# First token rows loaded as one tile of 48 rows; turned tokens split into fp16 parts straight from PSUM

## The chip, the cores and the metric

The kernel runs on one core of a Trainium2 chip. The metric is the device time of one execution in microseconds (us), the median of several runs. A core has five engines that run side by side, each in the order of its own instruction stream: PE (TensorE, matrix products and transposes into PSUM; PEld is its loading of the stationary operand), DVE (VectorE), ACT (ScalarE), POOL (GpSimd) and SP (SyncE, which here only issues DMAs). ACT issues DMAs too, and POOL. TensorE's clock has two levels, 1.2 and 2.4 GHz; the profile gives the granted share, 0.5 or 1.0.

## The reference, cut to what matters

One inference step of a one-layer mixer over 16 meta tokens, 32 sample tokens and 512 prompt tokens of width 2048:

```python
hn   = rmsnorm(h, pre_norm_w)                  # every token row, over 2048 features
proj = einsum('btd,de->bte', hn, w_in)         # 2048 -> 8192: q|f|i|gate | B|C|x|gate
...  # group A: gated linear recurrence over the tokens; group B: width-3 convolution
mix  = einsum('bte,ed->btd', concat(o, yb), w_out)
h    = h + rmsnorm(mix, post_norm_w)
```

The change touches only the way from the token rows `h` in HBM to the turned (feature-major) and normed tokens `hn` in SBUF, the right operand of the first product.

## The kernel before, in words

**Tokens.** The 560 tokens are worked on in two halves of 280 columns: per half 8 meta tokens and 16 sample tokens (24 "first" rows) and 256 prompt rows. The first rows lie in the tile `xs` of 56 rows, the second half's 24 from row 32 on (L105); rows 24 to 31 are never loaded, and so the whole tile is cleared first (L119). Six loads of 8 rows each, issued on ACT's DMA queue (L177 to 180), bring them in. The 512 prompt rows lie in four tiles `xp0` to `xp3` of 128 rows (L181 to 189), on SP's DMA queue between the first weights.

**Weights.** `w_in` comes in blocks of 1024 by 128 in float32 (`raw`, six buffers). For each pair of column blocks there are four: keys "11", "12", "21", "22" (first digit: column block; second: which half of the 2048 rows). `squares` (L249) sums their squares on ACT, `scale_of_weights` (L255) turns the sum into a power-of-two scale, with a small product `pss` on PE, and `split_w` (L273) writes a high fp16 part (ACT) and a low one (DVE).

**Norm.** `norm_x` (L348) squares one half of the features of a token tile on ACT and the other on DVE, works out the scale in small steps on DVE with one root on ACT, and scales the tile in place on DVE.

**Turning.** `turn_x(hf, k)` (L364), k from 0 to 15, turns 128 features of one half: three transposes on PE into one PSUM tile of 280 columns (24 + 128 + 128), an evacuation by ACT to the float32 tile `bf` (a view of `big`) with the norm weight as scale, and for every second k a cast of two k to the high fp16 part on POOL (L377) and a subtraction for the low part on DVE (L378). The results are `xo`, the x operand of all products (`x_b` in the trace). The PSUM tiles come from two pools of two buffers, so four are in flight.

**The product.** `plain` (L393) adds three fp16 matmuls for one k (high by high, high by low, low by high; L306 to 310). In the first loop (L397 to 406) `plain` runs `LAG` = 4 values of k behind `turn_x(0, k)`; at k = 3 the second weight block is split and at k = 6 `xp2` is normed. After it come the squares and splits of the two next weight blocks (L407 to 411), then a loop of `plain` with `turn_x(1, ...)` (L412) and another (L426). From there on the products of all other column blocks follow, then the output product.

**Order.** Everything that goes through `V`, `A`, `G`, `T` (DVE, ACT, POOL, PE) keeps the order of the program on its engine up to L432; DMA issues are placed by the framework's scheduler on their queue. `keep_busy` (L205) gives PE products of the identity without use, eight at the very start (L209) and eight more after `squares(0, ("11",))` (L384); they depend on no load.

Of the kernel before, what the change touches and what calls it, by code (L numbers as in the profile page):

```python
# [8 lines left out]
F32 = mybir.dt.float32  # L9
# [5 lines left out]
AF = mybir.ActivationFunctionType  # L15
ALU = mybir.AluOpType
# [3 lines left out]
P = 128  # L20
D = 2048
KT = D // P
SEQ = 512
# [13 lines left out]
KC = 8  # L37
TH = TOK // 2
# [23 lines left out]
def hymba_kernel(  # L62
# [14 lines left out]
    nc = tc.nc  # L77
    V, A, G, T = (_InOrder(tc, e) for e in (nc.vector, nc.scalar, nc.gpsimd, nc.tensor))
# [15 lines left out]
    bf = big.rearrange("p (h k t) -> p h k t", h=2, k=KT)  # L94
# [5 lines left out]
    def xop(n):  # L100
        return [xo[n][:, i] for i in range(2)]

    pre = ExitStack()
    xr = pre.enter_context(tc.tile_pool(name="xr", bufs=1))
    xs = xr.tile([56, D], F32, name="xs")  # L105
    xp = [xr.tile([P, D], F32, name=f"xp{i}") for i in range(4)]

    ident = const.tile([P, P], F32, name="ident")
    make_identity(nc, ident)
    epst = const.tile([P, 1], F32, name="epst")  # L110
    V.memset(epst, EPS)
    mask = const.tile([P, 8, W], U8, name="mask")
# [3 lines left out]
    wpr = xr.tile([16, P], F32, name="wpr")  # L116
    rest = const.tile([32, P], F32, name="rest")
    V.memset(rest, 0.0)
    V.memset(xs, 0.0)  # L119

    w2d = w_in[0]
    units = [(g * 1024 + i * P) for i in range(H) for pr in PAIRS for g in pr[0:2]]
# [1 line left out]
    raws = {}  # L124
# [7 lines left out]
    def load_w(p, key):  # L132

        i, j = int(key[0]) - 1, int(key[1]) - 1
        raw = wpool.tile([P, KC, P], F32, name=f"raw{key}_{p}", tag="raw", bufs=6)
        c0 = units[2 * p + i]
        src = w2d[j * KC * P:(j + 1) * KC * P, c0:c0 + P]
        nc.sync.dma_start(raw, src.rearrange("(k p) e -> p k e", p=P))
        raws[p, key] = raw
# [35 lines left out]

    xsm = x_sample.rearrange("b t d -> (b t) d").rearrange("(g h r) d -> h g r d", h=2, r=8)
    for hf in range(2):  # L177
        nc.scalar.dma_start(xs[32 * hf:32 * hf + 8], meta_tokens[8 * hf:8 * hf + 8])
        for g in range(2):
            nc.scalar.dma_start(xs[32 * hf + 8 + 8 * g:32 * hf + 16 + 8 * g], xsm[hf, g])  # L180
    nc.sync.dma_start(xp[0], x_prompt[0, 0:P])  # L181
    nc.sync.dma_start(wpr, pre_norm_w[0].rearrange("(r c) -> r c", c=P))
    load_w(0, "11")
    nc.sync.dma_start(xp[1], x_prompt[0, P:2 * P])
    load_w(0, "12")
# [14 lines left out]
    wsc = par[:, 96:112]  # L200
    sxk = par[:, 112:116]
    A.activation(par[:, 127:128], epst, AF.Sqrt)
    warm = ps_mm.tile([P, SEQ], F32, name="warm", tag="mm")

    def keep_busy(n):  # L205
        for _ in range(n):
            T.matmul(warm[:, 0:P], ident, ident, start=True, stop=True)

    keep_busy(8)  # L209
    pt = ps_o.tile([P, SEQ], F32, name="pt_pre", tag="o")  # L210

    def cw(j, c):
# [20 lines left out]
    def scale_of_tokens():  # L233


        t = par[:, 116:117]
        T.transpose(pt[:, 0:16], wpr, ident[0:16, 0:16])
        V.tensor_copy(wpre, pt[:, 0:16])
        V.tensor_reduce(t, wpre, axis=AX.X, op=ALU.max, apply_absolute_value=True)
        V.tensor_tensor(t, t, t, op=ALU.mult)  # L240
        T.transpose(pt[0:1, 128:256], t, ident)
        m = par[0:1, 117:118]
        V.tensor_reduce(m, pt[0:1, 128:256], axis=AX.X, op=ALU.max)
        T.matmul(pt[:, 256:257], ones[0:1, :], m, start=True, stop=True)
        power(sxk[:, 0:1], pt[:, 256:257], float(0x5F3759DF + (8 << 23)))
        V.tensor_scalar(wsc, wpre, sxk[:, 0:1], None, op0=ALU.mult)
        V.tensor_scalar(sxk[:, 1:2], sxk[:, 0:1].bitcast(I32), -1.0, float(381 << 23), op0=ALU.mult, op1=ALU.add)

    def squares(p, keys):  # L249
        t = sws.setdefault(p, wpool.tile([P, 8], F32, name=f"sq_{p}", tag="sq", bufs=4))  # L250
        for key in keys:
            c = ("11", "12", "21", "22").index(key)
            A.activation(junk, raws[p, key].rearrange("p k e -> p (k e)"), AF.Square, accum_out=t[:, c:c + 1])  # L253
# [94 lines left out]
    def norm_x(x, n, i):  # L348

        s0, z, r = rst[:n, 0, i:i + 1], rst[:n, 1, i:i + 1], rst[:n, 2, i:i + 1]  # L350
        A.activation(junk[:n], x[:, 0:D // 2], AF.Square, accum_out=ssp[:n, i, 0:1])
        V.scalar_tensor_tensor(junk2[:n], x[:, D // 2:D], 1.0, x[:, D // 2:D], op0=ALU.mult,
                               op1=ALU.mult, accum_out=ssp[:n, i, 1:2])
        V.tensor_tensor(s0, ssp[:n, i, 0:1], ssp[:n, i, 1:2], op=ALU.add)
        A.activation(r, s0, AF.Sqrt, bias=epst[0:n], scale=1.0 / D)
        V.tensor_scalar(z, s0, -0.5 / D, -0.5 * EPS, op0=ALU.mult, op1=ALU.add)
        V.reciprocal(r, r)
        V.scalar_tensor_tensor(z, r, z, r, op0=ALU.mult, op1=ALU.mult)
        V.scalar_tensor_tensor(r, z, 1.5, r, op0=ALU.add, op1=ALU.mult)
        for c in range(2):  # L360
            c = slice(c * D // 2, (c + 1) * D // 2)
            V.tensor_scalar(x[:, c], x[:, c], r, None, op0=ALU.mult)

    def turn_x(hf, k):  # L364
        pool, tag = ((ps_tr, "tr"), (ps_lv, "lv"))[k % 2]
        ps = pool.tile([P, SEQ], F32, name=f"xt{hf}_{k}", tag=tag)[:, 0:TH]
        ks = slice(k * P, (k + 1) * P)
        a = 32 * hf
        T.transpose(ps[:, 0:24], xs[a:a + 24, ks], ident[a:a + 24, a:a + 24])
        for b in range(2):  # L370
            T.transpose(ps[:, 24 + b * P:24 + (b + 1) * P], xp[2 * hf + b][:, ks], ident)
        A.activation(bf[:, hf, k, :], ps, AF.Copy, scale=wsc[:, k:k + 1])
        if k % 2:
            n = f"b{1 + k // KC}{1 + hf}"
            kk = slice((k - 1) % KC, (k - 1) % KC + 2)
            h, l = xop(n)
            G.tensor_copy(h[:, kk], bf[:, hf, k - 1:k + 1])  # L377
            V.tensor_tensor(l[:, kk], bf[:, hf, k - 1:k + 1], h[:, kk], op=ALU.subtract)  # L378

    scale_of_tokens()  # L380
    norm_x(xs, 56, 0)
    norm_x(xp[0], P, 1)
    squares(0, ("11",))
    keep_busy(8)  # L384
    norm_x(xp[1], P, 2)
    squares(0, ("12",))
    sc0 = scale_of_weights(0, (0, 2))
# [5 lines left out]
    def plain(o, a, hf, k):  # L393
        xn = f"b{1 + k // KC}{1 + hf}"
        mmk(o, ws[0, f"{a}{1 + k // KC}"], xop(xn), k % KC, 0, k == 0, k == KT - 1)

    LAG = 4  # L397
    for k in range(KT + LAG):
        if k < KT:
            turn_x(0, k)  # L400
        if k == 3:
            split_w(0, "12", raws[0, "12"])
        if k == 6:
            norm_x(xp[2], P, 3)
        if k >= LAG:
            plain(f0[0], "1", 0, k - LAG)
    squares(0, ("21", "22"))  # L407
# [4 lines left out]
    for k in range(KT):  # L412
        plain(f0[1], "2", 0, k)
        if k >= 4:
            turn_x(1, k - 4)
        if k == 2:
            lt = ps_o.tile([P, SEQ], F32, name="pt_lb", tag="o")
            T.transpose(lt[:, 32:40], lbp, ident[0:8, 0:8])
            V.tensor_copy(lb, lt[:, 32:40])
# [6 lines left out]
    for k in range(KT):  # L426
        if k < 4:
            turn_x(1, 12 + k)
        if k in (4, 8, 12):
            next(steps1)()  # L430
        plain(f0[2], "1", 1, k)
    V, A, G, T = nc.vector, nc.scalar, nc.gpsimd, nc.tensor  # L432
# [453 lines left out]
    op = ctx.enter_context(tc.tile_pool(name="op", bufs=1, side="right"))  # L886
# [168 lines left out]
    for dp in range(ND):  # L1055
# [3 lines left out]
        for j in range(4 * dp, 4 * dp + 4):  # L1059
            pool, tag = ((ps_mm, "mm"), (ps_x, "x"))[j % 7 >= 3]  # L1060
# [83 lines left out]
```

## Time and profile before

| | us |
|---|---|
| median of 3 runs | 1107.26 (1104.17 to 1107.37) |
| the profiled execution, its own time | 1106.25 |
| span of its trace (first to last instruction) | 1104.5 |
| PE busy | 1045.8 (95%) |
| DVE busy | 585.1 (53%) |
| ACT busy | 525.1 (48%) |
| POOL busy | 89.0 (8%) |
| DMA, mean | 99 GB/s, 109.38 MB |

Times in rows are us from the span's start unless marked ns. "[5.15 <-DMA xs]" behind a row means that the engine stood still for 5.15 us before it and that this transfer ended last of what it waited for. SPq and ACTq rows are the issuing of a DMA, not its transfer.

### The profile page before, as it was taken

What the parts mean: (1) busy time and instruction counts of PE and PEld (TensorE: products, weight loads), DVE (VectorE), ACT (ScalarE), POOL (GpSimd) and SP (SyncE); (2) the same over time, 40 slices, a digit from 0 to 9 for tenths busy, and PEclk for the clock granted to TensorE, in tenths of its full rate; (3) what the DMA queues carried; (4) which work ended last, traced back from release to release, by engine and by line L of the source; (5) the groups of instructions that cost most, each with busy time, mean ns of one, the idle gap of its engine ahead of it and who ended that gap; (6) DMA issues with size and microseconds to landing.
All of it is one profiled execution on the core that took longest, in us unless ns stands there. A gap on an engine that the chain in (4) does not pass through costs nothing.

```text
span 1104.5 us, 20854 instructions
## 1 busy us (share of the span) xinstructions
PE 1045.8 (95%) x8639; PEld 893.8 (81%) x8639; DVE 585.1 (53%) x1403; ACT 525.1 (48%) x1012; POOL 89.0 (8%) x151
## 2 busy tenths in 40 slices
PE   2589999999999999999999999999999999999995
PEld 2357888888788888878888888888788799999995
DVE  2755564466447554743664565557546662223226
ACT  1568744554554455445544554564455152332323
POOL 0220000000001000100001010001000010000004
PEclk7689999999999999999999999999999999999998
DMA  9214423323422244235223333432253154222204
GB/s 261 78 41 129 120 77 97 98 77 80 115 77 78 80 127 130 56 85 143 77 77 98 96 77 80 115 93 63 78 154 98 57 183 164 88 96 88 66 1 162
DMA packets 156949, 109.38 MB, mean 99 GB/s; under 512 B 3745, under 2 KB 151378, under 8 KB 155782
## 3 DMA queue, kind: packets, MB, share of 16 engines
q1 hardware_dynamic: 152934, 92.90, 30.1%
q0 software_dynamic: 3680, 14.49, 4.1%
q8 instruction: 67, 1.10, 0.4%
q10 hardware_dynamic: 240, 0.66, 0.2%
q14 instruction: 28, 0.23, 0.1%
HBM read 98.79 MB, written 9.25 MB: 98 GB/s over the span
## 4 chain that ended last, share of the span: by engine, by line
PE 74%; DVE 12%; DMA 7%; ACT 4%; issue 2%; POOL 0%; SPq 0%; DVEq 0%; ACTq 0%; POOLq 0%
PE mm L308 17%; PE mm L310 16%; PE mm L309 16%; DMA raw<-in_w_in_dram 6%; PE omm L952 3%; PE omm L950 3%; PE omm L951 3%; PE omm L959 2%; PE omm L960 2%; PE omm L958 2%; DVE w L277 2%; PE xt L58 2%; PE mm L58 1%; DVE q L673 1%; DVE y L837 1%
## 5 line engine op out<-in xcount | busy, mean ns | idle before, releaser
L308 PE MATMUL mm<-x_b,w 128*128 128x272 f16 (+2 forms) x2000 | 560.8, 280 | 1.4 <-ACT f L325 1.4
L310 PE MATMUL mm<-x_b,w 128*128 128x272 f16 (+2 forms) x2000 | 560.1, 280 | 0.0
L309 PE MATMUL mm<-x_b,w 128*128 128x272 f16 (+2 forms) x2000 | 560.1, 280 | 0.0
L308 PEld LDWEIGHTS <-w 128*128 128x128 f16 x2000 | 195.6, 98 | 42.3 <-issue 4.8
L310 PEld LDWEIGHTS <-w 128*128 128x128 f16 x2000 | 195.6, 98 | 37.9
L309 PEld LDWEIGHTS <-w 128*128 128x128 f16 x2000 | 195.7, 98 | 35.6
L253 ACT ACTIVATE junk<-raw 128x1024 bf16<-128x1024 f32 x120 | 126.9, 1058 | 115.3 <-DMA raw<-in_w_in_dram 115.2
L277 DVE SCALAR_TENSOR_TENSOR w<-raw,sc,w 128x1024 f16<-128x1024 f32 x124 | 153.4, 1277 | 26.0 <-ACT w L276 25.8
L276 ACT ACTIVATE w<-raw,sc 128x1024 f16<-128x1024 f32 x124 | 133.5, 1142 | 21.4 <-DVE sc L231 19.5
L170 DVE TENSOR_TENSOR wl<-rawo,wh 128x1024 fp32r<-128x1024 f32 x32 | 39.2, 1225 | 81.4 <-ACT wh L169 80.7
L950 PE MATMUL omm<-mh,wh 128*128 128x288 f32 x256 | 76.0, 297 | 0.0
L952 PE MATMUL omm<-mh,wl 128*128 128x288 f32 x256 | 75.5, 295 | 0.0
L951 PE MATMUL omm<-ml,wh 128*128 128x288 f32 x256 | 75.3, 294 | 0.0
L958 PE MATMUL omm<-wh,mh 128*128 128x256 f32 x256 | 72.7, 284 | 0.0
L959 PE MATMUL omm<-wl,mh 128*128 128x256 f32 x256 | 71.4, 279 | 0.0
L960 PE MATMUL omm<-wh,ml 128*128 128x256 f32 x256 | 71.3, 278 | 0.0
L169 ACT CAST wh<-rawo 128x1024 fp32r<-128x1024 f32 x32 | 33.5, 1048 | 76.8 <-PE omm L959 70.2
L656 ACT COPY kc<-kb 128x256 f32<-128x256 f32 x48 | 19.5, 406 | 75.8 <-PE lv L660 54.1
L959 PEld LDWEIGHTS omm<-wl,mh 128*128 128x128 f32 x256 | 48.2, 188 | 0.0
L950 PEld LDWEIGHTS omm<-mh,wh 128*128 128x128 f32 x256 | 48.1, 188 | 0.1
L951 PEld LDWEIGHTS omm<-ml,wh 128*128 128x128 f32 x256 | 48.2, 188 | 0.0
L958 PEld LDWEIGHTS omm<-wh,mh 128*128 128x128 f32 x256 | 48.1, 188 | 0.1
(272 smaller groups left out, 1246.4 us busy)
## 6 DMA issues: line engine op xcount, KB each, us to landing
raw<-in_w_in_dram SPq DMA_DIRECT2D x128, 512.0 KB, 5.8
rawo<-in_w_out_dram SPq DMA_DIRECT2D x32, 512.0 KB, 3.4
xp<-in_x_prompt_dram SPq DMA_DIRECT2D x4, 1024.0 KB
s<-in_state_hgrn_dram POOLq DMA_DIRECT2D x8, 512.0 KB, 4.7
out_dram<-s POOLq DMA_DIRECT2D x8, 512.0 KB, 6.9
xres<-in_x_prompt_dram POOLq DMA_DIRECT2D x4, 1024.0 KB, 9.2
out_dram<-big SPq DMA_DIRECT2D x7, 256.0 KB, 2.5
wpo<-in_post_norm_w_dram POOLq DMA_DIRECT2D x4, 256.0 KB, 4.5
```

The costliest lines, as they stand in the source:

```text
L253: A.activation(junk, raws[p, key].rearrange("p k e -> p (k e)"), AF.Square, accum_out=t[:, c:c + 1])
L276: A.activation(w[:, 0], raw, AF.Copy, scale=s)
L277: V.scalar_tensor_tensor(w[:, 1].rearrange("p k e -> p (k e)"), raw.rearrange("p k e -> p (k e)"), s, w[:, 0].rearrange("p k e -> p (k e)" ...
L308: T.matmul(o, w[:, 0, k, :], xh, start=first, stop=False)
L309: T.matmul(o, w[:, 0, k, :], xl, start=False, stop=False)
L310: T.matmul(o, w[:, 1, k, :], xh, start=False, stop=last)
L950: T.matmul(o, wh[:, s_], mh[e][:, 0:SA], start=(e == 0), stop=False)
L951: T.matmul(o, wh[:, s_], ml[e][:, 0:SA], start=False, stop=False)
L952: T.matmul(o, wl[:, s_], mh[e][:, 0:SA], start=False, stop=(e == KT - 1))
L958: T.matmul(o, mh[e][:, s_], wh, start=(e == 0), stop=False)
L959: T.matmul(o, mh[e][:, s_], wl, start=False, stop=False)
L960: T.matmul(o, ml[e][:, s_], wh, start=False, stop=(e == KT - 1))
```

## The change

`xs` shrinks to 48 rows, 24 for each half, and is no longer cleared. Both halves' first rows are turned together: one transpose of 48 rows gives 48 columns, with the 24 that are wanted at columns 24 to 47; for half 0 a permutation `turned` (the identity with its two blocks of 24 exchanged) takes the identity's place. The prompt's columns follow at 48. The evacuation by ACT writes the high fp16 part directly, and DVE writes the low part from the same PSUM tile, for every k; POOL has no part in it, and `bf` is not used there. `LAG` becomes 2. The eight first `keep_busy` products are gone; the second batch becomes ten and reads the weight block "11". `wpr` (the pre-norm weight) is loaded ahead of `xp0`.

```diff
-    xs = xr.tile([56, D], F32, name="xs")
+    xs = xr.tile([48, D], F32, name="xs")
...
+    turned = xr.tile([48, 48], F32, name="turned")
+    for a in (0, 24):
+        G.tensor_copy(turned[:, 24 - a:48 - a], ident[0:48, a:a + 24])
...
-    V.memset(xs, 0.0)
...
-        nc.scalar.dma_start(xs[32 * hf:32 * hf + 8], meta_tokens[8 * hf:8 * hf + 8])
+        nc.scalar.dma_start(xs[24 * hf:24 * hf + 8], meta_tokens[8 * hf:8 * hf + 8])
         for g in range(2):
-            nc.scalar.dma_start(xs[32 * hf + 8 + 8 * g:32 * hf + 16 + 8 * g], xsm[hf, g])
+            nc.scalar.dma_start(xs[24 * hf + 8 + 8 * g:24 * hf + 16 + 8 * g], xsm[hf, g])
+    nc.sync.dma_start(wpr, pre_norm_w[0].rearrange("(r c) -> r c", c=P))
     nc.sync.dma_start(xp[0], x_prompt[0, 0:P])
-    nc.sync.dma_start(wpr, pre_norm_w[0].rearrange("(r c) -> r c", c=P))
...
-    def keep_busy(n):
+    def keep_busy(n, at=ident):
         for _ in range(n):
-            T.matmul(warm[:, 0:P], ident, ident, start=True, stop=True)
-
-    keep_busy(8)
+            T.matmul(warm[:, 0:P], at, ident, start=True, stop=True)
+
...
-        ps = pool.tile([P, SEQ], F32, name=f"xt{hf}_{k}", tag=tag)[:, 0:TH]
+        ps = pool.tile([P, SEQ], F32, name=f"xt{hf}_{k}", tag=tag)
         ks = slice(k * P, (k + 1) * P)
-        a = 32 * hf
-        T.transpose(ps[:, 0:24], xs[a:a + 24, ks], ident[a:a + 24, a:a + 24])
+        T.transpose(ps[:, 0:48], xs[:, ks], ident[0:48, 0:48] if hf else turned)
         for b in range(2):
-            T.transpose(ps[:, 24 + b * P:24 + (b + 1) * P], xp[2 * hf + b][:, ks], ident)
-        A.activation(bf[:, hf, k, :], ps, AF.Copy, scale=wsc[:, k:k + 1])
-        if k % 2:
-            n = f"b{1 + k // KC}{1 + hf}"
-            kk = slice((k - 1) % KC, (k - 1) % KC + 2)
-            h, l = xop(n)
-            G.tensor_copy(h[:, kk], bf[:, hf, k - 1:k + 1])
-            V.tensor_tensor(l[:, kk], bf[:, hf, k - 1:k + 1], h[:, kk], op=ALU.subtract)
+            T.transpose(ps[:, 48 + b * P:48 + (b + 1) * P], xp[2 * hf + b][:, ks], ident)
+        h, l = (t[:, k % KC] for t in xop(f"b{1 + k // KC}{1 + hf}"))
+        o, c = ps[:, 24:24 + TH], wsc[:, k:k + 1]
+        A.activation(h, o, AF.Copy, scale=c)
+        V.scalar_tensor_tensor(l, o, c, h, op0=ALU.mult, op1=ALU.subtract)
...
-    norm_x(xs, 56, 0)
+    norm_x(xs, 48, 0)
...
-    keep_busy(8)
+    keep_busy(10, raws[0, "11"][:, 0, :])
...
-    LAG = 4
+    LAG = 2
```

## Rows read from the trace of the kernel before

**Rows 1.** Page, parts 1 and 2: busy time by engine; PE over 40 slices.
```profile
PE 1045.8 (95%) x8639; PEld 893.8 (81%) x8639; DVE 585.1 (53%) x1403; ACT 525.1 (48%) x1012; POOL 89.0 (8%) x151
...
PE   2589999999999999999999999999999999999995
```

**Rows 2.** Busy time of each engine by stretch, first line: the columns.
```profile
core 0: us, PE busy (x) PEld busy (x) DVE busy (x) ACT busy (x) POOL busy (x), PEclk, DMA share, GB/s
0.00:25.70 25.70, 6.63 (x36) 5.92 (x37) 4.03 (x16) 1.53 (x3) 1.76 (x7) 0.77 0.94 264
...
37.80:48.00 10.20, 10.15 (x39) 5.97 (x40) 7.11 (x15) 6.99 (x13) 2.91 (x4) 0.50 0.37 103
...
62.40:68.30 5.90, 5.88 (x24) 3.43 (x25) 5.24 (x12) 1.83 (x3) 0.00 (x0) 0.50 0.27 89
```

**Rows 3.** Chain of work that ended last, 0 to 38 us: start, us, what.
```profile
2.71 15.97 DMA raw<-in_w_in_dram
...
18.70 6.78 DMA xs<-in_x_sample_dram
...
25.71 1.24 DVE junk L58 x2
...
37.84 4.28 PE xt L58 x15
```

**Rows 4.** Timeline of the start: start, us, engine, operation, out<-in, count.
```profile
1.16 0.42 SPq L182 DMA_DIRECT2D wpr<-in_pre_norm_w_dram  x1
1.38 1.76 DVE L58 MEMSET xs<- 56x2048 f32 x1 [0.38 <-issue]
...
3.18 0.57 ACTq L178 DMA_DIRECT2D xs<-in_meta_tokens_dram  x1
3.79 0.63 ACTq L180 DMA_DIRECT2D xs<-in_x_sample_dram  x2
...
8.73 0.67 DVE L58 TENSOR_SCALAR par<-par 128x1 int32<-128x1 int32 x4
...
16.02 2.95 ACTq L180 DMA_DIRECT2D xs<-in_x_sample_dram  x2
```

**Rows 5.** Timeline: third norm on DVE, squares of the second weight block on ACT.
```profile
33.34 1.22 DVE L58 SCALAR_TENSOR_TENSOR junk<-xp 128x1024 bf16<-128x1024 f32 x1
...
35.07 1.04 ACT L58 ACTIVATE junk<-raw 128x1024 bf16<-128x1024 f32 x1
```

**Rows 6.** Timeline: the two batches of `keep_busy` on PE.
```profile
2.81 3.79 PE L58 MATMUL warm<-ident 128*128 128x128 f32 x16 [2.81 <-POOL ident masks.py:199]
...
8.43 2.05 PE L58 MATMUL warm<-ident 128*128 128x128 f32 x16
```

**Rows 7.** Chain, first loop: one `plain` and one `turn_x`, early and late.
```profile
42.12 0.71 PE mm L58 x3
42.83 0.86 PE xt L58 x3
...
52.31 0.36 PE mm L58 x3
...
55.34 0.55 PE xt L58 x3
```

**Rows 8.** Timeline: DVE and PE in the first loop and after it.
```profile
39.58 1.28 DVE L58 SCALAR_TENSOR_TENSOR w<-raw,sc,w 128x1024 f16<-128x1024 f32 x1 [0.97 <-ACT w L58]
...
41.91 0.92 PE L58 MATMUL mm<-x_b,w 128*128 128x280 f16 x3
...
51.37 0.40 PE L58 MATMUL mm<-x_b,w 128*128 128x280 f16 x2 [1.18 <-DVE x_b L58]
...
62.41 1.81 PE L58 MATMUL mm<-x_b,w 128*128 128x280 f16 x7 [0.91 <-DVE w L58]
```

**Rows 9.** Groups by line and shape on DVE: busy us, mean ns, idle before.
```profile
L58 DVE TENSOR_TENSOR x_b<-big,x_b 128x560 f16<-128x560 f32 x16 | 12.2, 769 | 12.0 <-POOL x_b L58 12.0
...
L849 DVE SCALAR_TENSOR_TENSOR y<-mm,sc,y 128x272 f32<-128x272 f32 x16 | 7.9, 491 | 0.5 <-PE mm L310 0.5
```

## The prediction

> **What bounds the kernel now.** I read the page first: PE is busy for 95% of the span, and of its 40 slices only the first and the last are clearly short of full [rows 1]. A slice is 27.6 us. From the third on PE has no gaps to speak of, so a change to the tokens' way in is worth just the time by which it moves the steady part of PE forward or back; nothing behind it gives time back or takes any. I then cut the start into stretches: from 0 to 25.7 us PE does 6.6 us of work, and the DMA engines are busy at 0.94 of their time with 264 GB/s [rows 2]. The chain of waits shows what that stretch waits for [rows 3]: the last load of `xs`, issued at 18.70 us, lands 6.8 us later, at 25.5, and only at 25.71 does DVE begin the first norm. From there to the first transpose at 37.84 runs a chain of three norms on DVE: 12.1 us. So the first transpose, call its time M, is set by `xs`, the smallest of the loads, and not by the large ones: the second weight block "12", issued at 2.71, lands at 18.7 [rows 3].
>
> Why `xs` is so late stands in the timeline [rows 4]. DVE clears `xs` until 3.14, so ACT's first load is issued at 3.18, after SP has five large loads in the queues. Three are issued by then; the last two come at 16.02 and 18.70, each taking turns with others for a place in the queue.
>
> **The change, part by part.** *The loads.* Without the clearing (1.76 us) ACT can issue at about the time SP does, 0.7 us. Six issues at 0.3 to 0.6 us [rows 4] end near 3 us, unless some must wait, as three do now, for an earlier transfer to land. For when the last one lands I have two bounds. The near one: 6 times 64 KB is 0.39 MB, 1.5 us at 264 GB/s, so about 5 us. The far one: 6.8 us behind the last issue, as the row of today shows with the queues full [rows 3], so 9.8 us, or 11 with a wait for a place. DVE has to work out the norm weight's scale first, which ends at 9.40 now [rows 4]; it hangs on `wpr`, which is now first on SP's queue instead of second behind 1 MB, so I put that end at 7 to 8.5. The first norm then starts between 7 and 11; I take 8.9, since both bounds of the load lie around it, and get M = 8.9 + 12.1 = 21.0 by this chain, 19.1 to 23.1 at its ends.
>
> Two other chains reach M. `xp1` goes ahead of block "12" in the same queue. From the third norm's start to M are 37.84 - 33.34 = 4.5 us [rows 3, 5]. Ahead of the end of `xp1` lie 0.39 + 1.05 + 0.52 + 1.05 MB and part of a state of 0.5 MB, about 3.4 MB, at 264 GB/s 13 us and a start of 1.5: an estimate of 14.5, which gives M = 19.0. Block "12" lands between 16.5 (0.5 MB later) and 18.7 (today); its squares are 1.04 us on ACT, after which comes what today lies between the end of the third norm and M, some 0.7, plus 0.2 for reading the sum: M = 18.4 to 20.6 [rows 3, 5]. All three chains end close together, so an `xs` that is earlier still buys little. M = 21.0 against 37.84: **-16.8 us**, with ends at 18.6 (-19.2) and 23.3 (-14.5).
>
> At this place the Trainium skill (DMA: Bandwidth & Descriptors, section on queues, rings and completion order) has a rule: every DMA engine takes turns between the queues that have work for it. By it a 64 KB load on ACT's queue would not stand behind SP's; today's 6.8 us speak against so fair a share. By the rule alone `xs` would land at 5 us, the chain over block "12" would set M at 20.6, and the sum would be 0.4 us better.
>
> *The first loop* lasts from M to the end of the last `turn_x`: 55.89 - 37.84 = 18.05 us now [rows 3, 7]. Three things change it. (a) With a lag of 2 thirteen `plain` stand ahead of the last `turn_x` on PE instead of eleven: 2 x 0.36 = 0.7 us at the high clock, 1.4 at the low one [rows 7]. (b) PE may turn only three tiles, 3 x 0.86 = 2.6 us, before the first product, which needs the low part of tile 0. On DVE that lies behind the weight's low part, which ends at 40.86, 3.0 us after M [rows 8]; with 0.5 us of its own, 3.5. PE waits 0.9 us, where now the product starts at 41.91 with five tiles turned. (c) At k = 6 the norm of `xp2` occupies DVE for (33.34 - 25.71) / 2 = 3.8 us [rows 3, 5], and the low part of tile 7 waits behind it. PE's lead is two tiles, 2 x 0.91 at the high clock or 2 x 1.57 at the low; it waits 3.8 + 0.5 - 1.8 = 2.5 or 1.2 us, against 1.18 now [rows 8]. I take +0.6. Together +2.2, with ends at +4 (low clock throughout) and -1 (the waits for POOL's cast, gone now, were worth more than the rows name).
>
> The low part is a DVE operation out of PSUM on 280 elements. The nearest row is the one of L849, the same form out of PSUM on 272: 0.49 us [rows 9], so 0.5, and 32 x 0.5 = 16 us take the place of 12.2 us. Per tile 0.5 on DVE and as much on ACT stay under PE's 0.91 at the high clock; PE stays the bound outside (b) and (c), and the +4 us of DVE cost nothing. The Trainium skill (VectorE: DVE Perf Modes, rules for kernel authors) advises to copy a product out of PSUM first when many operations read it, which the old way did; here two read it. The rows agree: 1.8 ns per element out of PSUM against 1.4 [rows 9].
>
> *48 columns* instead of 24 in each first transpose: nothing if the load of the stationary operand sets its pace, and 24/280 of 0.55 us, 32 times, 1.5 us, if the columns do. I take +0.5.
>
> *Hidden.* The first eight `keep_busy` go from a PE that then waits for loads. The ten new ones are 20 passes at 0.24 us (3.79/16) or 0.13 (2.05/16) [rows 6], 2.6 to 4.7 us. They wait for block "11", and behind them on PE stand the small product of the scale and the first transpose; with the block there by 12 they end by 17, before M. Were it there at 17, they would cost the time past 21. Two small copies for `turned` go to POOL, busy 1.8 of 25.7 us [rows 2]; only the transposes need them. `wpr` ahead delays `xp0` by one issue, 0.4 us [rows 4], inside the DVE chain. Behind the loop the same squares and splits follow, 62.41 - 55.89 = 6.5 us [rows 7, 8], and the second half's loops run PE without gaps.
>
> **Sum.** -16.8 + 2.2 + 0.5 = -14.1 us. The profiled execution took 1106.25 (span 1104.5), so 1092.1; the median of the runs is 1.0 above that one, so **1093**. The forecast's own bounds: -19.2 - 1 = -20.2, and -14.5 + 4 + 1.5 = -9.
>
> **Rivals.** *Clock high from M on.* The granted clock is 0.5 from 37.8 to 48 and again from 62.4 to 68.3 [rows 2]. In the first 25.7 us its mean is 0.77, so it was 1.0 for about 13.9 us and fell some 3.4 us after PE's last product at 10.5 [rows 2, 6]. If block "11" comes late, the ten products end less than that before M and the loop starts at 1.0. The 10.15 us of PE work in that stretch [rows 2] shrink by 0.55/0.86 to 6.5, -3.7, of which the waits of (b) and (c) take back about 1: 1090. The Trainium skill (TensorE: Matmul & The Clock Gate, part 1) has it that an idle array is throttled and activity frees it, which is what the ten products would use; the two batches of today agree, 0.24 and 0.13 us a pass. For it: the batch is tied to a load and so nearer to M. Against it: from 17 to 21 is still a longer rest than the one after which it fell.
>
> *`xs` still held up.* Two of the six loads wait for a place until a large load has landed, and then lie 6.8 us behind it. With the first megabyte in at about 6 us, the last lands at 13, M = 13 + 12.1 + 0.3 = 25.4: -12.4 + 2.7 = -9.7, or -7 if the place comes free later: 1097 to 1100. For it: three of six wait so today [rows 4].
>
> *No move.* The clearing was not what held `xs`; the queues do it just as long, and M stays at 37.8: +2.7, 1110. Against it: three of the six were issued the moment the clearing ended.
>
> *Slower through DVE.* The loops become DVE's if one low part out of PSUM takes longer than PE's 0.91 us per tile; each tile then costs the excess, 32 times. It eats the 14 us from 0.91 + 14/32 = 1.35 us on; at 1.6 it is 22 us: 1115. Against it: the 0.49 us of L849 [rows 9].
>
> **How the numbers follow.** Forecast 0.58, clock 0.12, `xs` held up 0.20, no move 0.05, slower through DVE 0.02; 0.03 for a gain lost later, between the forecast and no change. The range 1086 to 1100 takes in the first three and their bounds. A measurement of this kernel can tell some 0.3%, 3.3 us, from no change: faster 0.91, same 0.03, slower 0.06.
>
> **What would show it.** First norm on DVE at 7 to 11 us, first transpose at 19 to 23; from there to the last `turn_x` 19 to 21 us, with PE waiting for DVE once near the start and once at the norm of `xp2`; the low part at 0.5 us; from then on the same trace, shifted. An issue of `xs` on ACT after 6 us would make the prediction wrong, and so would a first loop over 24 us.

## The result and the profile after

The changed kernel takes 1111.92 us against 1107.35 (medians of 18 executions each); the ratio over all of them is 1.0055, with a 95% interval of 1.0032 to 1.0078. Forecast were 1093 us and a gain. Its profiled execution took 1109.12 us, span 1107.3, which is 2.9 us above the profile of before. It is the third shortest of the 18, of which five took 1118 to 1121 us, so the medians lie further apart than the two profiles.

The page, with the lines that answer to [rows 1]: PE is busy for 7 us more; the first slice is as empty as before, the second is fuller (0.7 instead of 0.5).

```profile
PE 1052.8 (95%) x8627; PEld 896.1 (81%) x8627; DVE 586.4 (53%) x1418; ACT 525.6 (47%) x1012; POOL 77.3 (7%) x137
...
PE   2789999999999999999999999999999999999995
```

The timeline of the start, for [rows 3 to 6] (start, us, engine, line, operation, out<-in, count):

```profile
0.72 0.60 ACTq L180 DMA_DIRECT2D xs<-in_meta_tokens_dram  x1
...
1.35 0.63 ACTq L182 DMA_DIRECT2D xs<-in_x_sample_dram  x2
...
3.35 0.28 ACTq L180 DMA_DIRECT2D xs<-in_meta_tokens_dram  x1
...
8.27 8.60 ACTq L182 DMA_DIRECT2D xs<-in_x_sample_dram  x2
...
12.79 4.63 PE L58 MATMUL warm<-ident,raw 128*128 128x128 f32 x20 [6.81 <-DMA raw<-in_w_in_dram]
...
22.43 1.22 DVE L58 SCALAR_TENSOR_TENSOR junk<-xs 48x1024 bf16<-48x1024 f32 x1 [15.55 <-DMA xs<-in_x_sample_dram]
...
34.66 0.31 PE L58 MATMUL xt<-turned,xs 48*128 48x48 f32 x1 [0.16 <-issue]
```

ACT issues three loads of `xs` by 2 us, now that nothing is cleared. The fourth comes at 3.35, and the last two at 8.27 and 16.58 (8.27 + 8.60 less the 0.28 of one issue). The first norm begins at 22.43 and the first transpose, M, at 34.66: 3.2 us earlier than before instead of 16.8. The chain of waits names what the sixth issue waited for, and shows one `plain` and one `turn_x` of the loop (start, us, what), for [rows 3, 7]:

```profile
2.10 14.46 DMA xp<-in_x_prompt_dram
16.58 5.62 DMA xs<-in_x_sample_dram
...
42.73 0.70 PE mm L58 x3
43.44 0.90 PE xt L58 x3
```

`xp1`, issued at 2.10, lands at 16.56, and 0.02 us later the sixth load of `xs` is issued; it lands at 22.2. The stretches of the start, first line the columns, for [rows 2]:

```profile
core 0: us, PE busy (x) PEld busy (x) DVE busy (x) ACT busy (x) POOL busy (x), PEclk, DMA share, GB/s
...
34.60:44.80 10.20, 9.68 (x36) 5.39 (x36) 5.88 (x12) 5.37 (x10) 0.24 (x1) 0.50 0.24 68
44.80:59.20 14.40, 14.02 (x54) 7.95 (x54) 7.72 (x18) 5.25 (x13) 0.00 (x0) 0.50 0.09 26
...
69.20:83.40 14.20, 14.20 (x94) 9.39 (x95) 10.06 (x23) 8.78 (x19) 0.00 (x0) 1.00 0.15 43
```

The same for the kernel before, from 48 us on:

```profile
48.00:58.50 10.50, 8.60 (x59) 5.67 (x58) 6.13 (x9) 6.06 (x13) 3.54 (x5) 0.99 0.01 2
```

From M to the end of the last turn at 59.14 the first loop takes 24.5 us instead of 18.0. PE is busy for 23.7 of them, at granted clock 0.5 throughout; before, the clock stood at 1.0 from about 48 us on. The whole difference of the spans, 2.8 us, is thus: M -3.2, the loop +6.4, from its end to the next full run of products 0.0 (6.5 us both times), the second half up to its last turn -0.6, the rest +0.2.

### The profile page after: what moved, and what is told of

It is laid out like the page before. It is cut to its first block, busy times and chain, and to the rows that moved or that the text cites. A ratio compares the mean times of both kernels' runs of the same rounds, so it can differ in the third digit from the quotient of the medians.

```text
span 1107.3 us, 20831 instructions
## 1 busy us (share of the span) xinstructions
PE 1052.8 (95%) x8627; PEld 896.1 (81%) x8627; DVE 586.4 (53%) x1418; ACT 525.6 (47%) x1012; POOL 77.3 (7%) x137
## 4 chain that ended last, share of the span: by engine, by line
PE 75%; DVE 13%; DMA 6%; ACT 4%; issue 2%; POOL 0%; SPq 0%; DVEq 0%; ACTq 0%
PE mm L309 17%; PE mm L311 16%; PE mm L310 16%; DMA raw<-in_w_in_dram 4%; PE omm L949 3%; PE omm L948 3%; PE omm L947 3%; PE omm L956 2%; PE omm L957 2%; PE omm L955 2%; DVE w L278 2%; PE xt L58 2%; PE mm L58 2%; DMA xp<-in_x_prompt_dram 1%; ACT w L277 1%
```

## The experiments

**The changed kernel once more.** No edit.

> The changed kernel itself once more, for a second trace. In its profile the first transpose is at 34.66 us (37.84 before), the first loop takes 24.5 us to the end of the last turn (18.05 before), and the granted clock is 0.5 throughout the loop. Theory Q (places): the last two loads of xs wait for the landing of xp0 and xp1, so the first transpose stands at 33 to 36 us in every execution and the gain ahead of it is only about 3 us. Theory C (clock): the loop is long because the clock stays low, which may fall out otherwise in another execution: then the loop takes 17 to 19 us and the whole 1103 to 1106. If the loop is short and the whole is still 1109 or more, both lack something.

Measured: 1110.84 us, 1.0053 of before (1.0027 to 1.0079). M stands at 34.90, the loop takes 24.5 us. The clock record of this profile lacks its beginning, but the chain has 0.89 us for each turn and 0.70 for each product up to 59.4, the durations of the low clock. So neither M nor the loop is chance; both want a cause.

**`lag4`: the lag alone back.**

```diff
-    LAG = 2
+    LAG = 4
```

> The changed kernel with LAG 4 in place of 2. Theory L (lag): the shorter lead lets PE wait for DVE more often and puts more products ahead of the last turn; with 4 the first loop takes 2 to 4 us less, the median falls to 1108 to 1110. Theory C (clock): the lag matters only through the clock; if the clock rises within the loop as before (10 us after its start), the loop falls from 24.5 to 18 to 19 us and the median to 1104 to 1106; if it stays low, it is 23 to 24 us and the median 1111. Theory Q (places) expects the first transpose unmoved at 34.7.

Measured: 1106.62 us, 1.0011 of before (0.9985 to 1.0036); 4.2 us less than with LAG 2 beside it, and below theory L's 1108 to 1110. The stretches of the first loop, of the time behind it and of the second half's turns (columns as above):

```profile
34.90:56.80 21.90, 21.90 (x82) 12.37 (x83) 13.39 (x30) 10.49 (x20) 0.24 (x1) 0.50 0.17 49
58.70:62.10 3.40, 1.12 (x9) 0.68 (x8) 0.95 (x6) 2.14 (x4) 0.41 (x2) 1.00 0.01 2
62.10:66.80 4.70, 3.98 (x17) 1.83 (x16) 4.28 (x10) 2.23 (x4) 0.00 (x0) 0.50 0.31 112
66.80:91.10 24.30, 24.30 (x93) 13.99 (x93) 10.66 (x24) 8.90 (x18) 0.00 (x0) 0.50 0.09 25
```

The loop is 2.6 us shorter, and PE now stands still nowhere in it; the clock is low all the same. Theory L holds for these 2.6 us, theory C's hope for the clock does not; where the other 1.6 us of the medians come from is not shown. This profile is of one of the longer executions, 1115.23 us, and its last row says why: the second half's turns ran at the low clock too, 24.3 us where the changed kernel's profile above has 14.2 at the high one. The clock had risen behind the loop, stood at 1.0 for a stretch in which PE mostly waited, and was low again when the next products began.

**`oldbusy`: the useless products as before.**

```diff
+    keep_busy(8)
...
-    keep_busy(10, raws[0, "11"][:, 0, :])
+    keep_busy(8)
```

> The changed kernel with the two batches of eight useless products as before (products of the identity at the very start and behind the squares of the first weight block) instead of one of ten on the landed block. Theory B (batch): the ten products or their place are to blame; the median falls to 1104 to 1106. Theories L and Q: nothing, 1110 to 1113, first transpose at 34 to 35 us, since both batches end long before it.

Measured: 1110.07 us, 1.0037 (1.0021 to 1.0054). M 34.74, loop 24.5:

```profile
34.70:59.20 24.50, 23.62 (x88) 13.30 (x89) 13.57 (x30) 10.60 (x20) 0.24 (x1) 0.50 0.15 44
```

The batch makes no difference that these runs can tell, as was forecast; it ends at 17.4, 17 us before M.

**`twoqueues`: the loads of `xs` on two queues.**

```diff
+        q = (nc.sync, nc.scalar)[hf]
-        nc.scalar.dma_start(xs[24 * hf:24 * hf + 8], meta_tokens[8 * hf:8 * hf + 8])
+        q.dma_start(xs[24 * hf:24 * hf + 8], meta_tokens[8 * hf:8 * hf + 8])
...
-            nc.scalar.dma_start(xs[24 * hf + 8 + 8 * g:24 * hf + 16 + 8 * g], xsm[hf, g])
+            q.dma_start(xs[24 * hf + 8 + 8 * g:24 * hf + 16 + 8 * g], xsm[hf, g])
```

> The changed kernel with the three xs loads of the first half issued on SP's queue ahead of everything there and the other three on ACT's. Theory Q (places): all six are then among the first eight transfers and none waits for a large one; xs is in SBUF by 6 to 9 us, the first transpose at 20 to 23 us instead of 34.7, and the median 10 to 13 us lower, 1098 to 1102. If the first transpose moves and the whole does not, the time is lost later. If xs still lands at 20 us, the places were not what held it.

Measured: 1097.24 us, 0.9934 of before (0.9905 to 0.9962); 13.6 us below the changed kernel on the same chip. Timeline of the start, and the loop:

```profile
0.72 0.60 ACTq L181 DMA_DIRECT2D xs<-in_meta_tokens_dram  x1
0.73 0.40 SPq L181 DMA_DIRECT2D xs<-in_meta_tokens_dram  x1
1.18 0.62 SPq L183 DMA_DIRECT2D xs<-in_x_sample_dram  x2
1.35 0.62 ACTq L183 DMA_DIRECT2D xs<-in_x_sample_dram  x2
...
8.32 1.06 ACT L58 ACTIVATE junk<-xs 48x1024 bf16<-48x1024 f32 x1 [4.81 <-DMA xs<-in_x_sample_dram]
...
11.62 1.22 DVE L58 SCALAR_TENSOR_TENSOR junk<-xs 48x1024 bf16<-48x1024 f32 x1
...
23.90:48.30 24.40, 23.55 (x88) 13.22 (x89) 13.50 (x29) 10.60 (x20) 0.24 (x1) 0.50 0.41 117
```

All six are issued by 2 us and have landed at 8.3. M is at 23.86, 10.8 us earlier than in the changed kernel's first profile and 11.0 earlier than in `again`. The lead is still 11.1 us at the second half's last turn; the spans differ by 15.7 us, and for the rest, behind that turn, no run shows a cause: there the profiles of this document vary between 1021.2 and 1025.8 us.

Theory Q is shown: the loads were held by the places. In both kernels eight transfers of SP's and ACT's queues are issued without a wait and the ninth is not; by the semaphores in the trace each later one waits until the earlier transfer whose place it takes has landed. In the changed kernel the fourth `xs` load takes the place of the first (landed 3.33, issued 3.35), the fifth that of `xp0` (8.24 and 8.27), the sixth that of `xp1` (16.56 and 16.58). The Trainium skill (DMA: Bandwidth & Descriptors, section on issuing engines not being separate DMA queues) says that a second issuing engine saves only the time of issuing, usually little. Both kernels here issue on both engines; moving three loads to SP was worth 10.8 us of M because it brought the small loads ahead of the large ones in the row for a place. No run has all six ahead of the large loads on one queue. The first norm now waits for the norm weight's scale (`wpr`, issued behind the `xs` loads, lands at 8.3), which ends at 11.6.

**`tq_lag4`: two queues and LAG 4.** Both edits above.

> The changed kernel with the xs loads on two queues and LAG 4 besides. The two gains, 13.6 us for the loads and 4.2 us for the lag in the medians of the first runs, should add if they sit in different stretches: first transpose at 23.9 us, loop 21.9 us at the low clock, median 1092 to 1094. If the lag acts only through the clock's luck, it stays at 1096 to 1098.

Measured: 1100.17 us, 0.9939 (0.9909 to 0.9969). M 23.81, loop 21.9. The times lie in two groups of equal size, 1093.4 to 1097.3 and 1103.1 to 1104.3; the profile is of the upper one:

```profile
23.80:45.70 21.90, 21.89 (x82) 12.50 (x83) 13.43 (x30) 10.48 (x20) 0.24 (x1) 0.50 0.46 130
55.70:80.00 24.30, 24.30 (x93) 14.00 (x93) 10.71 (x24) 8.88 (x18) 0.00 (x0) 0.50 0.09 25
```

The second row again: turns and products without a gap on PE for 24 us, and the clock never rises. The lower group, around 1095, lies a little above the 1092 to 1094 of the sum. Half of the executions are some 8 us longer; the one of them that was profiled lost 10 us to the clock in the second half.

**`tq_lag4_warm`: useless products just ahead of the first transpose.** On top of `tq_lag4`:

```diff
-    keep_busy(10, raws[0, "11"][:, 0, :])
     norm_x(xp[1], P, 2)
+    keep_busy(8, xp[0][:, 0:P])
```

> The same with the useless products moved: eight, on the normed rows of xp0, so that they run in the last 4 us before the first transpose. Theory C (clock): in all five traces of the changed forms the loop ran at granted clock 0.5 from its first to its last instruction; if it starts at 1.0 it takes 15 to 18 us instead of 21.9, and the median is 3 to 6 us below that of tq_lag4, 1087 to 1090. If the clock falls back within the loop, 1090 to 1093. Theory D (DVE out of PSUM is the bound): nothing changes, the loop stays at 21 to 22 us.

Measured: 1095.86 us, 0.9922 (0.9901 to 0.9943). The products, the first turns (timeline), and three stretches:

```profile
18.96 3.78 PE L58 MATMUL warm<-ident,xp 128*128 128x128 f32 x16 [7.99 <-DVE xp L58]
...
25.93 0.44 PE L58 MATMUL xt<-ident,xp 128*128 128x128 f32 x2
27.48 0.34 PE L58 MATMUL xt<-turned,xs 48*128 48x48 f32 x1 [1.12 <-DVE x_b L58]
...
23.10:26.50 3.40, 2.44 (x13) 1.35 (x12) 1.82 (x7) 1.96 (x4) 0.42 (x2) 1.00 1.06 368
26.50:45.90 19.40, 18.42 (x70) 10.66 (x71) 12.01 (x26) 8.41 (x17) 0.00 (x0) 0.50 0.40 101
```

The clock was high at M (24.09), stayed so for four turns without a product between them, and fell; the rest of the loop ran at 0.5, and it took 21.8 us. So here a high clock at M was not kept to the first products. PE also waited 1.0 us ahead of the four turns and 1.1 behind them; turns and waits are not told apart. The expected gain in the loop did not come. The median is below that of `tq_lag4`, within its lower group, which the loop does not explain; one of the ten executions is as long as the upper group, instead of five.

**`before_split`: the kernel before with the split from PSUM alone.**

```diff
-        A.activation(bf[:, hf, k, :], ps, AF.Copy, scale=wsc[:, k:k + 1])
-        if k % 2:
...
+        A.activation(h, ps, AF.Copy, scale=c)
+        V.scalar_tensor_tensor(l, ps, c, h, op0=ALU.mult, op1=ALU.subtract)
```

> The kernel before with one part of the change alone: the high part written by ACT and the low part by DVE straight from PSUM for every k; xs of 56 rows, 24-column transposes, LAG 4 and loads as before. Theory S (the split costs): the DVE step out of PSUM is what makes the loop long; 22 us or more and the median 3 to 5 us above before, 1109 to 1111. Theory T (48 columns): the split is harmless, the clock rises some 10 us into the loop as before, the loop takes 17 to 19 us and the median is 1104 to 1106, because what keeps the clock low is the longer turn of 48 columns (0.89 us against 0.86) beside products of 0.70.

Measured: 1104.59 us, 0.9991 of before (0.9972 to 1.0010): the split alone neither gains nor costs. Its loop in two stretches:

```profile
36.70:46.90 10.20, 10.13 (x39) 5.91 (x40) 7.65 (x17) 6.58 (x13) 0.24 (x1) 0.50 0.36 105
46.90:56.90 10.00, 10.00 (x46) 6.04 (x45) 5.61 (x13) 3.84 (x10) 0.00 (x0) 0.59 0.00 0
```

PE doesn't wait for DVE anywhere, so theory S falls. The clock rises inside the loop, at 55, some 18 us after its start; 20.2 us in all, which is more than theory T's 17 to 19, because the rise came later than the 10 us of before.

**`before_lag2`: the kernel before with LAG 2 alone.** `LAG = 2`, nothing else.

> The kernel before with LAG 2 in place of 4 and nothing else. Theory L (lag): the shorter lead alone costs; two more products ahead of the last turn and waits for the low part, loop 20 to 25 us in place of 18, median 2 to 5 us above before, 1108 to 1111. If it is the combination with the split that costs, median within 1 us of before.

Measured: 1115.17 us, 1.0083 of before (1.0051 to 1.0114), more than any theory gave; the loop takes 28.5 us. Its chain:

```profile
54.30 0.63 PE mm L58 x2
54.93 0.86 PE xt L58 x3
55.81 0.50 ACT big L58
56.37 0.66 POOL x_b L58
57.05 0.75 DVE x_b L58
57.84 0.62 PE mm L58 x2
```

With the parts made for two k at a time, a lead of two lets PE, ACT, POOL and DVE work one after the other: 3.54 us for two tiles from product to product. The split for every k is what makes a lag of 2 bearable: with it the lag costs 2.6 us in the loop (`again` against `lag4`, both at the low clock), without it 10.5. Part of the 10.5 is the clock, which the durations show low to the end of this loop (0.86 us a turn).

**`cols24`: the changed kernel with 24-column transposes.** `xs` has 56 rows again; the rows between the halves are filled by a load of 16 instead of 8 rows, and the halves start at 0 and 32.

```diff
-        T.transpose(ps[:, 0:48], xs[:, ks], ident[0:48, 0:48] if hf else turned)
+        T.transpose(ps[:, 0:24], xs[a:a + 24, ks], ident[a:a + 24, a:a + 24])
...
+            nc.scalar.dma_start(xs[16:32], x_sample.rearrange("b t d -> (b t) d")[16:32])
```

> The changed kernel with the first transposes back at 24 columns (xs of 56 rows, the rows between the halves filled by one longer load instead of a clearing), all else as changed: loads, LAG 2, split from PSUM. Theory T (48 columns): the longer turn (0.89 us against 0.86) keeps the clock low through the loop; with 24 the clock rises within it in a good part of the executions, the loop falls from 24.5 to 19 to 22 us, the median by 2 to 4 us to 1107 to 1109. Theory L (lag): the columns cost only their own 0.03 to 0.05 us per turn, 0.5 us in the loop and 1 to 1.5 in all; loop 23.9 to 24.1, median 1109 to 1110.

Measured: 1107.63 us, 1.0014 of before (0.9998 to 1.0030); the changed kernel had 1.0053. The loop, now with a mean clock above 0.5, and products at three places of its timeline:

```profile
36.30:59.40 23.10, 20.56 (x89) 12.17 (x90) 13.48 (x30) 10.39 (x21) 0.24 (x1) 0.85 0.16 46
...
45.66 0.91 PE L58 MATMUL mm<-x_b,w 128*128 128x280 f16 x3
...
48.20 0.52 PE L58 MATMUL mm<-x_b,w 128*128 128x280 f16 x3
...
51.25 0.62 PE L58 MATMUL mm<-x_b,w 128*128 128x280 f16 x2 [1.85 <-DVE x_b L58]
```

The 0.85 leans on a record that begins only at 47; the durations are those of the low clock up to there (a turn 0.85 us, a product 0.70). From 47.4 to 50.8, some 11 us into the loop, the clock is high (the three matmuls of a product take 0.52 in the timeline instead of 0.91). PE then waits 1.85 us for DVE, the clock is low again from 50.8, and it rises once more at 57.6, before the last two turns (0.54 and 0.36). The loop is 1.4 us shorter than in `again`, and M stands 1.4 us later (36.26), so the start as a whole gains nothing in this profile. What the twelve executions lack is a group of long ones: they lie between 1105.6 and 1109.6.

**`tq_cols24`: two queues, LAG 4, 24 columns.** The edits of `twoqueues`, `lag4` and `cols24`.

> The form with the xs loads on two queues and LAG 4, with 24-column transposes. Theory T: of ten to fifteen executions fewer fall into the upper group at 1103 to 1104 in which the second half's turns run at the low clock (five of ten with 48 columns), median 1092 to 1095. Theory L: as with 48 columns, two groups half and half, about 1 us lower each.

Measured: 1090.38 us, 0.9869 of before (0.9843 to 0.9894), all executions between 1089.2 and 1094.4. Loop at both levels, and the second half's turns:

```profile
25.10:40.30 15.20, 15.13 (x58) 8.88 (x59) 11.42 (x26) 8.45 (x16) 0.24 (x1) 0.50 0.68 191
40.30:44.00 3.70, 3.70 (x27) 2.47 (x25) 1.89 (x4) 1.98 (x5) 0.00 (x0) 1.00 0.00 0
53.90:67.60 13.70, 13.70 (x93) 9.23 (x93) 9.23 (x20) 8.55 (x17) 0.00 (x0) 1.00 0.08 21
```

The clock rises 15 us into the loop, which takes 18.9 us instead of 21.9 with 48 columns, and no execution of the six lies above 1103. That is theory T: the median is 9.8 us below that of `tq_lag4`, and some 5 us below that form's lower group; the columns' own time (0.89 less 0.85 us, 32 times) is 1.3. The two forms ran on different chips, each beside the kernel before, and how large the upper group is in ten executions may differ; the loops are one profile each.

**`tq_lag8` and `tq_cols24_lag8`: LAG 8**, with 48 and with 24 columns.

> The form with the xs loads on two queues, 48 columns, and LAG 8. If the lag costs by the products that stand ahead of the last turn on PE (0.70 us each at the low clock), four fewer make the loop 2.8 us shorter than with LAG 4, 19.1 us, and the eight left over run while ACT squares and splits the next weights, 6.5 us in which PE stood still: median 1090 to 1093, and a longer unbroken row of products after the loop also lets the clock rise before the second half, so that the upper group at 1103 to 1104 goes. If the gain of the lag ends at 4, the median is that of LAG 4, 1093 to 1100.

> All three together: xs loads on two queues, 24 columns, LAG 8. By the sum of the terms 1089 to 1092; if the columns only cost their own time, 1 us below tq_lag8.

Measured: 1092.44 us, 0.9887 (0.9858 to 0.9915), and 1091.07, 0.9875 (0.9849 to 0.9901). First the loop, the gap behind it and the second half with 48 columns, then the loop's two levels with 24:

```profile
24.00:43.40 19.40, 19.23 (x70) 10.75 (x71) 13.28 (x30) 10.16 (x20) 0.24 (x1) 0.50 0.51 143
43.40:53.10 9.70, 6.95 (x45) 4.45 (x43) 4.89 (x15) 6.11 (x10) 0.41 (x2) 0.85 0.17 54
53.10:68.10 15.00, 15.00 (x94) 9.71 (x94) 10.90 (x23) 8.83 (x19) 0.00 (x0) 0.94 0.14 41
```

```profile
24.70:36.10 11.40, 11.33 (x42) 6.36 (x42) 9.57 (x23) 8.20 (x16) 0.24 (x1) 0.50 0.89 249
36.10:40.70 4.60, 4.33 (x30) 2.91 (x30) 3.45 (x8) 1.97 (x4) 0.00 (x0) 0.99 0.01 4
```

With 48 columns the loop is 2.6 us shorter than with LAG 4, close to the 2.8 that were worked out. The clock rises behind it, at 44.7, falls at 51.5 and rises again 2 us into the second half; five of the six executions lie between 1091.0 and 1092.9 and one at 1099.5. That the longer row of products is what keeps most of them short is not shown. With 24 columns the loop falls to 16.1 us, but the whole isn't measurably below `tq_cols24`: the intervals cover each other, and no run says where its 2.8 us of loop went. `tq_cols24` and the two LAG 8 forms lie 12 to 15 us below the kernel before.

## Why the prediction was wrong, point by point

**What bounds the kernel** was right in the main: M is set by the last load of `xs` and 12.2 us of norms behind it (22.43 to 34.66; 12.1 were taken), and a shift of M is paid out in full (`twoqueues`: 11.0 us of M, 11.1 at the second half's last turn). But "nothing behind it gives time back or takes any" was not: the start reaches to that turn at 83 us. In [rows 1] not the first slice alone but the first three are short of full (2, 5 and 8 tenths), and the second half's turns can take 14 us or 24.

**The step that failed first is the term for M**, -16.8, measured -3.2. I took the landing of the last load from its issue, and put all issues near 3 us "unless some must wait"; the far bound left room for a last issue at some 4 us (11 less 6.8), the rival for a wait behind one large load. The rows held the answer: three of six loads waited before, though SP and ACT issue side by side [rows 4], and the last began when a large load had landed. Taking the clearing away moved the first issue from 3.18 to 0.72, but the row for a place stayed: the fifth load waits for `xp0` and the sixth for `xp1`, 16.6 us. Had I counted the transfers ahead of the sixth load, I would have had its issue at the landing of `xp1`, for which I had an estimate of 14.5, plus 6.8 and 12.1: M = 33.4. The rival "`xs` still held up" named the mechanism and gave it a place behind the first megabyte; it was behind the second. `twoqueues` shows what the term would have been without that wait: M 23.9, which is -14.0 and 0.5 us outside the bounds that were given for it (18.6 to 23.3), because the first norm then waits until 11.6 for the norm weight's scale. The rival "no move" came nearest with its 1110. It said that the queues hold `xs` as long without the clearing, which is so for the last load; that its total is near 1111.92 is luck, for M did move, by 3.2 us, and the loop took more than it gave. Two readings beside this were off: SP had four large loads and the small `wpr` in the queues, not five large ones [rows 4], and the ends 18.6 and 23.3 of the term are not those of the chain over `xs`, 19.1 and 23.1.

**The second step is the loop**, +2.2 with a bound of +4, measured +6.4. Its parts, by one profile each: the lag 2.6 (`again` against `lag4`, at the low clock), for which the forecast had 2.2; the 48 columns 3.1 (`tq_lag4` against `tq_cols24`), of which I had seen only their own time, up to 1.5 for all 32; the remaining 0.8 lies between `tq_cols24` and before, the split among it. That 2.2 is near 2.6 is in part luck: the two products more cost 1.4 us at the low clock instead of 0.7, and PE stood still for 0.8 us in all (24.5 less 23.7) where the waits alone were to grow by 1.5. As far as the profiles show, the columns cost by way of the clock. In all eight profiles with 48 columns the clock stayed at 0.5, or fell to it, to the loop's end; in all five with 24 columns and a PE without long waits it rose within it, 10 to 18 us after M (`before_lag2` has the long waits, and there it stayed low). I had taken the rise 10 us into the loop before as given, and let only a low clock "throughout" stand as a bound. That bound was too small by its own rows: 16 x 0.86 + 13 x 0.71 [rows 7] are 23.0 us without any wait, 4.9 above the 18.05 of before.

**The columns and the clock once more in the second half**: no more than the columns' own time was forecast, +0.5 in all. Of 84 executions of the changed forms with 48 columns 19 lie more than 6 us above the fastest of their form, of 24 with 24 columns none. Two of the 19 were profiled (`lag4`, `tq_lag4`), and in both the second half's turns stayed at the low clock, 24.3 us instead of 14 to 15. With 24 columns a low clock at the start of these turns did not last: it rose after 5 us in `cols24` and after 9 in `before_split`.

**Right**: the low part out of PSUM, 0.5 us forecast, and in the profile after, for [rows 9]:

```profile
L58 DVE SCALAR_TENSOR_TENSOR x_b<-xt,par,x_b 128x280 f16<-128x280 f32 x32 | 15.7, 506 | 13.9 <-ACT x_b L58 13.7
```

Hidden as forecast: the ten products (12.79 to 17.42, and `oldbusy`), the copies for `turned`, the stretch behind the loop (6.5 us). "Slower through DVE" did not come; nothing in the changed loop waits long for DVE (PE busy 23.7 of 24.5 us). The rival "clock high from M on" was wrong twice: the batch ends 17 us before M, and in `tq_lag4_warm` a high clock at M fell after four turns. Its reading that the clock before was 1.0 for the first 13.9 us is wrong as well: the first batch took 0.24 us a pass, the low clock's time, and only the second 0.13 [rows 6].

The rule of the Trainium skill (TensorE: Matmul & The Clock Gate, part 1) that activity frees the clock does not carry this loop as it was read: PE was busy for 21.90 of 21.90 us in `lag4`, two thirds of them with transposes (16 x 0.89), and the clock stayed low. The measurement decides.

**Open**: why 24 columns more, 0.04 us per turn, decide whether the clock rises. The profiles, eight against five, show that it goes with the columns; beside the columns the loads of `xs` differ a little, and M by 1.3 us. Nor is it shown when a row of products lifts the clock: behind the two rows ahead of the second half it rose at 69.2 in the profile after, behind the same two rows in `lag4` (63.33 to 66.85) it did not.

## What to carry to other kernels

Before a load is called early, count the transfers that are issued ahead of it: when issues wait for a place, a small load late in the row can start only when a large one lands (here at 16.6 us), whatever frees its own engine. Loads that everything waits for belong among the first, on both queues if need be. Where PE alternates transposes and products, read the granted clock of that stretch in the profile first: here 24 columns more, a few hundredths of a microsecond per turn, went with another level for most of the stretch. A forecast then needs both levels as its bounds, each worked out with all other terms.

## What the runs showed of the hardware

TensorE at 100% busy can stay at the low clock for 24 us (`lag4`, `tq_lag4`: turns of 0.89 us and products of 0.70 in turn, granted 0.5), while the same row of work, begun at the high clock, kept it (69.20 to 83.40 in the profile after: granted 1.00). The clock can also be granted while PE mostly waits, and be gone when the work comes (`lag4`: 1.00 from 58.7 to 62.1, 0.50 for the products behind). A load of 64 KB on eight rows took 5.6 us from its issue to its landing with the queues full (16.58 to 22.2), though it is some 4% of the 1.69 MB that moved in that time (301 GB/s over 5.62 us).
